# Two expert layers in a written order, with regrouped gather and scatter, contiguous weight loads, and attention products by halves

## The chip, the cores and the metric

The kernel runs on one core of a Trainium2 chip. The metric is the device time of one execution in microseconds (us); lower is better. TensorE is PE in the profile (its weight loads PEld), VectorE is DVE, ScalarE is ACT, GpSimd is POOL, and SyncE is SP, which issues most transfers. PE's clock is granted at one of two levels, 1.2 or 2.4 GHz; the profile shows the granted share of 2.4 GHz.

## What is computed

A sequence of 512 tokens of width 1024 goes through two layers of a first block and then through a second block. A layer of the first block is a mixer (grouped attention, a bidirectional state-space scan, differential attention and a spatial gate, joined by four gates), an expert layer, and a gated addition of a per-layer embedding (ple). The second block is a forgetting attention (fox), a convolutional feed-forward layer, a gated recurrence (hgrn) and a second feed-forward layer. The change is mostly in the expert layer:

```python
affinity = jax.nn.softmax((h @ w_router).astype(jnp.float32), axis=-1)
top_aff, idx = lax.top_k(jnp.swapaxes(affinity, 1, 2), cap)      # cap = 64 tokens for each of 16 experts
xe = h[bidx, idx]
hid = jax.nn.silu(jnp.einsum('becd,edf->becf', xe, w_gate_e)) * jnp.einsum('becd,edf->becf', xe, w_up_e)
ye = jnp.einsum('becf,efd->becd', hid, w_down_e)
return jnp.zeros_like(h).at[bidx, idx].add(ye * top_aff[..., None].astype(ye.dtype))
```

Each expert has three float32 matrices of 1024 x 1024, so a layer reads 48 of them, 192 MiB.

## The kernel before, in words

The activations lie in on-chip memory as eight tiles `x[j]` of 128 features by 512 tokens. Dense layers outside the experts split each float32 operand into a high and a low float32r part and sum three products, 512 columns wide. The expert matrices are multiplied in float32 without a split; the profile counts a float32 product as two records.

**Routing** (`route`, L1518). PE transposes the logits, DVE and ACT form the softmax, and DVE takes the 64 best tokens of each expert in eight rounds. Meanwhile PE turns `x` into token rows, and ACT scales them into eight tiles `ht[t, q]` (L1548). The result `pos_t` holds each token's slot at each expert.

**Pairs.** The experts go in eight pairs. `onehot(p)` (L1589) compares the slots with 1 to 64 and gives a 0/1 matrix of 512 tokens by 128 (two experts of 64). `gather` multiplies `ht` by it in float32: for each of eight feature chunks, four products of 128 columns. `product` (L1654) multiplies the gathered rows, 64 columns of stationary operand for each of the two experts e, with the matrices; the two experts write the two halves of PE's columns and run beside each other. Gate and up are 64 records each, and so are the two halves of down together (`half`, L1667). `down` (L1704) transposes the 0/1 matrix, weighs the result into a high and a low part (`yy`: ACT, then DVE), and scatters it: for each `x[j]`, two products of 512 columns and one addition by DVE (`add_x`).

**Loads.** `raw` (L1637) fetches 1 MiB at a time into a ring: 11 slots of `xraw`, 4 of `xraw2`, 2 of `raw`, and 3 that are used once, for loads 5 to 7 of a layer. A pair takes 24 loads, eight for each matrix kind. Gate and up loads take 256 rows of a matrix, so a partition gets two runs of 4 KiB; down loads take 512 rows of half the columns, four runs of 2 KiB. Before the last two downs the ring is closed and opened with 5 slots.

**Order.** `tc.manual_schedule()` keeps the program's order on every engine. In `moe` it covers only the routing and the first gather (L1586); behind it, a scheduler with its own cost estimates orders the instructions of each engine, so loads and small pieces move ahead of others. The mixer, `ple`, fox and hgrn are in a manual order that a planner writes (`Runner.go` with a `Clock` of estimated costs). `ple_early` (L1752) prepares products for the next stage and is a generator, advanced between the last halves of down.

**Attention.** `gqa` (L1059) builds operands by `halves`: a tile whose partitions 0 to 63 and 64 to 127 hold two parts of a head, copied by transfers on SP (`put`). A score is a 128-row product plus a 64-row one with the low part of k. In fox's `score` (L1881) each of two heads hh takes three 64-row products and a mask, first one head and then the other.

Of the kernel before, what the change touches and what calls it, by code (L numbers as in the profile page):

```python
# [21 lines left out]
S = 512  # L22
# [515 lines left out]
class Net:  # L538
# [520 lines left out]
    def gqa(self, i, aq, akv, rope):  # L1059
# [6 lines left out]
        for a, x in enumerate(tl):  # L1066
# [7 lines left out]
            st, low = self.halves(x, a == 0)  # L1074
            both.append(st)
            if a == 0:
                kl = low
            yield
        out = []
        sk, sq = both[0], both[1:]  # L1080

        def score(u):
            if u.qc == 0:
                u.g.po = self.psum("po")
            rows = slice(u.g.n * 64, (u.g.n + 1) * 64)
# [432 lines left out]
    def route(self, X, wk, t2k):  # L1518

        nc, ident, lg = self.nc, self.ident, X.lg  # L1520
        rt = lambda: t2k()[:NE]
        ps = self.xnorm_sums(X)
        zero = rt()
        nc.gpsimd.memset(zero, 0.0)
# [17 lines left out]
        def rows(t, q):  # L1542
# [8 lines left out]
        tq = [(t, q) for t in range(NT) for q in range(2)]  # L1551
        some = [(t, q, rows(t, q)) for t, q in tq[:2]]
# [5 lines left out]
        for t, q in tq[2:]:  # L1558
            normed(t, q, rows(t, q))
        aT = rt()  # L1560
# [6 lines left out]
        mk, cs = rt(), rt()  # L1567
        nc.vector.tensor_scalar(mk, aT, 0.0, None, op0=OP.is_lt)
        nc.vector.tensor_tensor_scan(cs, mk, zero, 0.0, op0=OP.add, op1=OP.add)
# [11 lines left out]
    def moe(self, i, X, nxt):  # L1581
        yield
        nc, I = self.nc, self.I
        with self.phase(X, {"mm": 4, "sm": 2, "po": 2}) as wk, self.work(f"ring_{X.name}", X.side) as px2, ExitStack() as top:
            t2k = lambda dt=F32: self.t(wk, [128, S], dt, "t2k", 11)
            with self.tc.manual_schedule():  # L1586
                af, ht, pos_t = self.route(X, wk, t2k)

                def onehot(p, n=1):  # L1589

                    o = t2k()
                    ov = o.rearrange("p (t e s) -> p t e s", t=NT, e=2)
                    for t in range(0, NT, NT // n):
                        sl = slice(t, t + NT // n)
                        nc.vector.tensor_tensor(ov[:, sl], pos_t[:, sl, 2 * p:2 * p + 2][:, :, :, None].to_broadcast([128, NT // n, 2, CAP]),
                                                self.c("slot")[:, None, None, :].to_broadcast([128, NT // n, 2, CAP]), op=OP.is_equal)
                    return lambda t: o[:, t * 128:(t + 1) * 128]

                def gather(i, oh, n=1):

                    xe = {}

                    def part(q, n=1):
                        ps = self.psum("sm")
                        for k in range(4):
                            for t in range(NT):
                                self.mm(ps[:, k * 128:(k + 1) * 128], ht[t, q][:, k * 128:(k + 1) * 128], oh(t),
                                        start=t == 0, stop=t == NT - 1)
                        x = xe[q] = t2k()
                        xv, pv = (v.rearrange("p (k c) -> p k c", k=4) for v in (x, ps))  # L1610
                        for k in range(0, 4, 4 // n):
                            sl = slice(k, k + 4 // n)
                            nc.vector.tensor_tensor(xv[:, sl], pv[:, sl], self.sm(f"g_moe{i}", 4 * q + k, 4 // n)[:, :, None].to_broadcast([128, 4 // n, 128]),
                                                    op=OP.mult)

                    def stat(k, e):
                        if k // 4 not in xe:
                            part(k // 4)
                        return xe[k // 4][:, (k % 4) * 128 + e * 64:(k % 4) * 128 + e * 64 + 64]
                    if n > 1:  # L1620
                        part(0, n)
                    return stat
                oh = onehot(0, 4)
                start = oh, gather(i, oh, 4)


            seq, once = [0, 0], range(5, 8)
            place = Box(pool=top.enter_context(self.work(f"first_{X.name}", X.side)))

            def settle():  # L1630
                top.close()
                place.pool = top.enter_context(self.work(f"late_{X.name}", X.side))
# [45 lines left out]
            def hidden(p):  # L1678
# [6 lines left out]
                if p == 0:  # L1685
                    settle()
# [608 lines left out]
```

## Time and profile before

| | |
|---|---|
| runs of before, median (lowest to highest) | 3641.29 us (3637.7 to 3650.09), 3 runs |
| the profiled execution, its time | 3644.31 us |
| its span | 3642.5 us |
| mean granted clock | 0.976 |
| PE busy | 3438.2 us (94%) |
| DVE, ACT, POOL busy | 1748.7 (48%), 1103.5 (30%), 276.5 (8%) |
| float32 products of the experts (four groups), busy by single records | 431.0 + 225.7 + 71.2 + 62.2 us |
| moved by transfers | 632.53 MB, mean 174 GB/s |

A busy PE means that some product is in flight; products overlap, so busy time is not the time at PE's peak. DMA share is the busy share of 16 transfer engines, and can read slightly over 1. In rows of windows the columns are: window, its length, then busy time (and instructions) of PE, PEld, DVE, ACT and POOL, then the granted clock, the DMA share and GB/s. L196 is the helper line through which every instruction goes, so groups are told apart by the tiles that they write and read (`mm`, `sm`, `po` are accumulators of the products, of gather and scatter, and of the transposes). The first expert layer lies at about 600 to 1130 us, the second at about 1740 to 2260 us, and fox at 2317 to 2615 us.

### The profile page before, as it was taken

How to read it: one execution, taken by the hardware profiler on the slowest of the kernel's cores; microseconds unless marked ns; L12 is line 12 of the kernel's file. 1: busy time of each engine (PE TensorE's matmuls, PEld its weight loads, DVE VectorE, ACT ScalarE, POOL GpSimd, SP SyncE). 2: the span in 40 equal slices, each digit the busy share in tenths (PEclk: the TensorE clock that was granted, in tenths of full speed). 3: DMA queues.
4: the chain of work that ended last, by engine and by line, in shares of the span. 5: the costliest groups of instructions: out<-in, count | busy, mean ns of one | idle time of the engine just before them, and what ended most of it. 6: DMA issues, size and time to landing. Idle time of an engine off the chain costs nothing.

```text
span 3642.5 us, 42086 instructions
## 1 busy us (share of the span) xinstructions
PE 3438.2 (94%) x17170; PEld 2422.3 (67%) x17170; DVE 1748.7 (48%) x2976; ACT 1103.5 (30%) x1754; POOL 276.5 (8%) x162
## 2 busy tenths in 40 slices
PE   7999878999999999988999999999999999999998
PEld 6787665434446777766444444777788888978887
DVE  4566853111116546764111113644565566667555
ACT  3443321000014344322000002444443344434333
POOL 0011320000001000221000000211100000000000
PEclk9999988999999999999999999999999999999999
DMA  5241336999983332236899986222222332213322
GB/s 158 81 129 60 102 124 260 386 382 403 397 334 99 103 90 88 83 97 255 315 378 397 392 347 219 88 76 73 67 94 93 104 94 80 64 64 100 98 93 81
DMA packets 346432, 632.53 MB, mean 174 GB/s; under 512 B 20008, under 2 KB 192552, under 8 KB 346240
## 3 DMA queue, kind: packets, MB, share of 16 engines
q1 hardware_dynamic: 330672, 613.53, 46.9%
q10 hardware_dynamic: 15568, 16.32, 1.5%
q8 instruction: 135, 2.21, 0.3%
q14 instruction: 57, 0.47, 0.0%
HBM read 618.15 MB, written 4.31 MB: 171 GB/s over the span
## 4 chain that ended last, share of the span: by engine, by line
PE 50%; DVE 5%; ACT 1%; issue 0%; DMA 0%; DVEq 0%; ACTq 0%
PE mm L196 41%; PE sm L196 3%; PE po L196 2%; PE s L196 1%; DVE x L196 1%; PE t L196 1%; DVE pl L196 1%; PE a L196 1%; DVE ach L196 1%; DVE w L196 0%; DVE t2k L196 0%; DVE sg L196 0%; ACT ach L196 0%; DVE P L196 0%; DVE yy L196 0%
## 5 line engine op out<-in xcount | busy, mean ns | idle before, releaser
L196 PE MATMUL mm<-ach,ph 128*128 128x512 f32 x5504 | 1751.1, 400 | 72.5 <-DVE w L196 46.4
L196 PEld LDWEIGHTS mm<-ach,ph 128*128 128x128 f32 x5504 | 1026.8, 191 | 317.3 <-issue 63.1
L196 PE MATMUL mm<-ach,pl 128*128 128x512 f32 x2752 | 1084.8, 394 | 0.6 <-DVE pl L196 0.5
L196 PEld LDWEIGHTS mm<-ach,pl 128*128 128x128 f32 x2752 | 523.7, 190 | 115.0 <-DVE pl L196 1.7
L196 ACT CAST ph<-raw 128x1024 fp32r<-128x1024 f32 (+1 forms) x366 | 373.6, 1030 | 301.7 <-PE mm L196 265.4
L196 PE MATMUL mm<-xraw,t2k 128*64 128x512 f32 x1840 | 431.0, 595 | 11.1 <-DVE t2k L196 11.1
L196 DVE TENSOR_TENSOR pl<-raw,ph 128x1024 fp32r<-128x1024 f32 (+1 forms) x317 | 390.6, 1235 | 96.7 <-ACT ph L196 94.7
L196 PEld LDWEIGHTS mm<-xraw,t2k 128*64 128x64 f32 x1840 | 140.0, 137 | 263.5 <-issue 234.0
L196 PE MATMUL mm<-xraw,hT 128*64 128x512 f32 x848 | 225.7, 598 | 0.0
L196 POOL TENSOR_TENSOR pl<-raw,ph 128x1024 fp32r<-128x1024 f32 x49 | 120.2, 2453 | 801.3 <-ACT ph L196 691.5
L196 DVE TENSOR_TENSOR t2k<-sm,small 128x512 f32<-128x512 f32 (+1 forms) x38 | 22.5, 606 | 307.0 <-PE mm L196 205.8
L196 ACT ACTIVATE w<-w 128x512 f32<-128x512 f32 x130 | 80.1, 629 | 283.8 <-DVE w L196 271.5
L196 ACT ACTIVATE sg<-mm 128x512 f32<-128x512 f32 x32 | 19.0, 597 | 416.9 <-PE mm L196 416.8
L196 PEld LDWEIGHTS sm<-t2k,t2k 128*128 128x128 f32 x1024 | 125.0, 203 | 21.8 <-issue 13.0
L196 PEld LDWEIGHTS mm<-xraw,hT 128*64 128x64 f32 x848 | 64.0, 136 | 109.7 <-issue 108.8
L196 PE MATMUL sm<-t2k,t2k 128*128 128x128 f32 x1024 | 130.9, 289 | 3.1 <-DVE t2k L196 1.6
L196 DVE SCALAR_TENSOR_TENSOR y<-u,small,y 128x512 f32<-128x512 f32 x176 | 131.9, 749 | 3.1
L196 DVE SCALAR_TENSOR_TENSOR yy<-mm,ac,yy 128x512 fp32r<-128x512 f32 x32 | 24.0, 751 | 220.4 <-ACT yy L196 220.4
L196 PE MATMUL sm<-oT,yy 128*128 128x512 f32 x256 | 90.9, 456 | 39.9 <-ACT yy L196 22.9
L196 DVE TENSOR_TENSOR sg<-sg,mm 128x512 f32<-128x512 f32 x32 | 21.9, 688 | 204.0 <-PE mm L196 204.0
L196 DVE TENSOR_TENSOR w<-mm,R 128x512 f32<-128x512 f32 x92 | 63.1, 688 | 113.9 <-PE mm L196 106.6
L196 POOL TENSOR_TENSOR w<-w,w 128x512 f32<-128x512 f32 x64 | 96.2, 1515 | 273.0 <-DVE w L196 263.4
(302 smaller groups left out, 3411.2 us busy)
## 6 DMA issues: line engine op xcount, KB each, us to landing
xraw<-in_w_exp_gate_dram SPq DMA_DIRECT2D x116, 1024.0 KB, 14.1
xraw<-in_w_exp_up_dram SPq DMA_DIRECT2D x114, 1024.0 KB, 18.5
xraw<-in_w_exp_down_dram SPq DMA_DIRECT2D x106, 1024.0 KB, 13.4
raw<-in_ffn_w_up_dram SPq DMA_DIRECT2D x44, 1024.0 KB, 5.1
raw<-in_w_branch_gate_dram SPq DMA_DIRECT2D x32, 1024.0 KB, 5.3
raw<-in_w_in_dram SPq DMA_DIRECT2D x22, 1024.0 KB, 5.4
raw<-in_w_exp_down_dram SPq DMA_DIRECT2D x22, 1024.0 KB, 11.0
raw<-in_ffn_w_down_dram SPq DMA_DIRECT2D x16, 1024.0 KB, 4.9
```

The source lines that it names most:

```text
L196: r = g(*a, **kw)
```

## The change

- The expert layer is in manual order throughout. The first 16 loads stand ahead of the routing in the program.
- The routing leaves `ht` as a high and a low float32r part (ACT scales, ACT copies, POOL subtracts), feature half by feature half.
- The 0/1 matrix covers four experts (256 columns), and the gather for two pairs is eight chunks of four times two float32r products of 256 columns.
- The scatter sums two pairs in one accumulation, so `add_x` comes half as often, and it stands behind the next gate product.
- The expert matrices are laid out so that a load of 1 MiB is one contiguous run of 8 KiB for each partition. Down goes through `product` except for the last pair.
- The ring has 1 slot of `xraw2` instead of 4; the once-used slots take loads 4 to 6; `ple_early` runs in one piece.
- gqa's second score product is 128 rows, from two more tiles (four more `put` transfers for each layer); fox's products alternate between the two heads.

```diff
-    def halves(self, x, twice):
-
-        h, l = self.parts(x)
+    def halves(self, x, order):
...
-        for g in range(2):
-            own, other = slice(g * 64, (g + 1) * 64), slice((1 - g) * 64, (2 - g) * 64)
-            o = self.w2k(F32R)
-            self.put(o[own], h[own])
-            self.put(o[other], (h if twice else l)[own])
-            out.append(o)
-        return out, l
+        for a, b in order:
+            row = []
+            for g in range(2):
+                own, other = slice(g * 64, (g + 1) * 64), slice((1 - g) * 64, (2 - g) * 64)
+                o = self.w2k(F32R)
+                self.put(o[own], parts[a][own])
+                self.put(o[other], parts[b][own])
+                row.append(o)
+            out.append(row)
+        return out
-            st, low = self.halves(x, a == 0)
-            both.append(st)
-            if a == 0:
-                kl = low
+            both.extend(self.halves(x, ((0, 1),) if a else ((0, 0), (1, 1))))
...
-        sk, sq = both[0], both[1:]
+        sk, sl, sq = both[0], both[1], both[2:]
...
                 self.mm(ps[r], q[:, cols], sk[u.g.n], start=True, stop=False)
-                self.mm(ps[r], q[rows, cols], kl[rows, :], start=False, stop=True)
+                self.mm(ps[r], q[:, cols], sl[u.g.n], start=False, stop=True)
...
-        def normed(t, q, ps):
-            o = ht[t, q] = t2k()
-            nc.scalar.activation(o, ps, AF.Identity, scale=r[:, t:t + 1])
+        def normed(q, t, ps):
+            h, l, f = t2k(F32R), t2k(F32R), t2k()
+            nc.scalar.activation(f, ps, AF.Identity, scale=r[:, t:t + 1])
+            nc.scalar.copy(h, f)
+            nc.gpsimd.tensor_tensor(l, f, h, op=OP.subtract)
+            ht[t, q] = h, l
...
-        with self.phase(X, {"mm": 4, "sm": 2, "po": 2}) as wk, self.work(f"ring_{X.name}", X.side) as px2, ExitStack() as top:
-            t2k = lambda dt=F32: self.t(wk, [128, S], dt, "t2k", 11)
+        with self.phase(X, {"mm": 4, "sm": 2, "po": 2}) as wk, self.work(f"ring_{X.name}", X.side) as px2, ExitStack() as top, \
+                self.tc.manual_schedule():
+            t2k = lambda dt=F32: self.t(wk, [128, S], dt, "t2k", 20)
...
+            seq, once = [0, 0], range(4, 7)
...
-                    return self.raw(src, nk, 2 * D // nk)
-                v = v.rearrange("p (k n) -> p k n", k=nk)
-                nc.sync.dma_start(v, src.rearrange("(k p) n -> p k n", p=128))
-                return v
-
+                    v = self.t(self.praw, [128, 2 * D], F32, "raw", bufs=self.RAW)
+                nc.sync.dma_start(v, src)
+                return v.rearrange("p (k n) -> p k n", k=nk)
+            def loads(w, p):
+                return [[raw(w[2 * p + e, kk], 2) for e in range(2)] for kk in range(4)]
...
-                    rv = [raw(w[2 * p + e][kk * 256:(kk + 1) * 256], 2) for e in range(2)]
+                    r = rv[kk] if rv else [raw(w[2 * p + e, kk], 2) for e in range(2)]
...
-                    rv = [raw(w[2 * p + e][kk * 512:(kk + 1) * 512, m * 512:(m + 1) * 512], 4) for e in range(2)]
+                    rv = [raw(w[2 * p + e, 2 * m + kk], 4) for e in range(2)]
...
+            first = [loads(I["w_exp_gate"][i], 0), loads(I["w_exp_up"][i], 0)]
+            af, ht, pos_t = self.route(X, wk, t2k, lambda: late([128, S], F32, "rt", 2))
+            def onehot(g, n=1):
+                o = self.t(wk, [128, NT, 4 * CAP], F32R, "oh", 1)
+                ov = o.rearrange("p t (e s) -> p t e s", e=4)
+                for t in range(0, NT, NT // n):
+                    sl = slice(t, t + NT // n)
+                    nc.vector.tensor_tensor(ov[:, sl], pos_t[:, sl, 4 * g:4 * g + 4][:, :, :, None].to_broadcast([128, NT // n, 4, CAP]),
+                                            self.c("slot")[:, None, None, :].to_broadcast([128, NT // n, 4, CAP]), op=OP.is_equal)
+                return o
...
+            def gather(b, oh):
+                ps = self.psum("sm")
+                pv = ps.rearrange("p (k c) -> p k c", k=2)
+                for k in range(2):
+                    q, c = divmod((2 * b + k) * 128, 512)
+                    for t in range(NT):
+                        for a, part in enumerate(ht[t, q]):
+                            self.mm(pv[:, k], part[:, c:c + 128], oh[:, t], start=t == 0 and a == 0, stop=t == NT - 1 and a == 1)
+                x = xe[b] = t2k().rearrange("p (k c) -> p k c", k=2)
...
+            def returns(g, oh):
+                for p in (2 * g, 2 * g + 1):
+                    o = lambda t: oh[:, t, p % 2 * 128:(p % 2 + 1) * 128].bitcast(F32)
+                    po = self.psum("po")
+                    for t in range(NT):
+                        nc.tensor.transpose(po[:, t * 128:(t + 1) * 128], o(t), self.ident)
+                    oT = late([128, S], F32R, "oT", 2)
+                    nc.scalar.copy(oT, po)
+                    pa = self.psum("po")
+                    for t in range(NT):
+                        self.mm(pa[:, :2], o(t), af[:, t, 2 * p:2 * p + 2], start=t == 0, stop=t == NT - 1)
+                    ac = self.t(wk, [128, 1], F32, "ac", 3)
+                    for e in range(2):
+                        nc.vector.tensor_copy(ac[e * 64:(e + 1) * 64], pa[e * 64:(e + 1) * 64, e:e + 1])
+                    back[p] = oT, ac
+            def scatter(j):
+                ps = self.psum("sm")
+                sl = slice(j % 4 * 128, (j % 4 + 1) * 128)
+                mms = [(part[:, sl], oT) for ys, oT in group for part in ys[j // 4]]
+                for q, (y, oT) in enumerate(mms):
+                    self.mm(ps, y, oT, start=q == 0, stop=q == len(mms) - 1)
+                self.add_x(j, ps)
+            def scatters():
+                for j in range(ND):
+                    scatter(j)
+                group.clear()
+            def gate(p, **kw):
+                sg = []
+                pgs = product(I["w_exp_gate"][i], p, rows_of(p), **kw)
                 if p == 0:
-                    oh, xe = start
-                else:
-                    oh = onehot(p)
-                    xe = gather(i, oh)
-                gp = product(I["w_exp_gate"][i], p, xe)
-                if p == 0:
+                    top.close()
+                    place.pool = top.enter_context(self.work(f"late_{X.name}", X.side))
...
+                return sg
+            def up(p, sg, **kw):
+                for s, pg in zip(sg, product(I["w_exp_up"][i], p, rows_of(p), **kw)):
+                    nc.vector.tensor_tensor(s, s, pg, op=OP.mult)
+            def turn(sg):
...
+            def weigh(p, m, py, ys):
+                yh, yl = (late([128, 512], F32R, "yy", 8) for _ in range(2))
+                nc.scalar.activation(yh, py, AF.Identity, scale=back[p][1])
+                nc.vector.scalar_tensor_tensor(yl, py, back[p][1], yh, op0=OP.mult, op1=OP.subtract)
+                ys[m] = yh, yl
+            NP = NE // 2
+            oh = onehot(0, 4)
+            gather(0, oh)
+            sg = gate(0, between=lambda kk: gather(kk + 1, oh) if kk < 3 else None, rv=first[0])
+            up(0, sg, rv=first[1])
+            for p in range(NP):
+                hT = turn(sg)
+                if p + 1 < NP:
+                    if p % 2:
+                        for b in range(4):
+                            gather(b, oh)
+                    sg = gate(p + 1)
+                    if p % 2 == 0:
+                        if group:
+                            scatters()
+                        returns(p // 2, oh)
+                        if p + 2 < NP:
+                            oh = onehot(p // 2 + 1)
+                    up(p + 1, sg)
+                if p == NP - 2:
 
                     X.close_ring()
                     nxt.begin()
                     X.open_ring(X.last)
-                    early = self.ple_early(i, nxt, raw, t2k)
-                    next(early)
-                down(p, *hid, early)
-                hid = nxt_hid
+                    for _ in self.ple_early(i, nxt, raw, t2k):
+                        pass
+                ys = {}
+                if p < NP - 1:
+                    group.append((ys, back[p][0]))
+                    for m, py in enumerate(product(I["w_exp_down"][i], p, hT)):
+                        weigh(p, m, py, ys)
+                    continue
+                self.clock.sync()
+                for m in range(2):
+                    weigh(p, m, half(I["w_exp_down"][i], p, hT, m), ys)
+                    if m == 0:
+                        scatters()
+                        group.append((ys, back[p][0]))
+                    for j in range(4 * m, 4 * m + 4):
+                        scatter(j)
+                        if j == ND - 2:
+                            X.close_ring()
+                            nxt.prime(1)
+                        nxt.chunk(j)
...
-            ps = []
+            ps = [self.psum("s") for _ in range(2)]
...
+            for m, o in ((0, 0), (0, 1), (1, 0)):
+                for hh in range(2):
+                    rows = slice(hh * 64, (hh + 1) * 64)
+                    self.mm(ps[hh][:, :n], q[m][rows, cols], k[o][rows, :n], start=m + o == 0, stop=False)
-                ps.append(p)
+                self.mm(ps[hh][:, n - 128:n], self.identb, maskb, start=False, stop=True)
...
+    for k in ("w_exp_gate", "w_exp_up", "w_exp_down"):
+        v = inp[k]
+        a[k] = v.reshape(2, NE, 4, 2, 128, D).transpose(0, 1, 2, 4, 3, 5).reshape(2, NE, 4, 128, 2 * D)
+        if k == "w_exp_down":
+            u = v[:, NE - 2:].reshape(2, 2, 2, 4, 128, 2, D // 2).transpose(0, 1, 5, 2, 4, 3, 6)
+            a[k] = np.concatenate([a[k][:, :NE - 2], u.reshape(2, 2, 4, 128, 2 * D)], 1)
+    a["w_ple"] = inp["w_ple"].reshape(2, 2, 128, D).transpose(0, 2, 1, 3).reshape(2, 128, 2 * D)
...
-        X.append(AheadMoe(net, f"e{i}", "left", "right", i, 11, 5, 4))
+        X.append(AheadMoe(net, f"e{i}", "left", "right", i, 11, 5, 1))
```

## Rows read from the trace of the kernel before

**Rows 1.** Second part of the page: busy tenths in 40 slices of the span.

```profile
PE   7999878999999999988999999999999999999998
DMA  5241336999983332236899986222222332213322
```

**Rows 2.** Windows of both layers, first expert product to last up product; columns as on the page.

```profile
608.00:1057.00 449.00, 426.29 (x2117) 187.61 (x2115) 69.40 (x116) 30.77 (x50) 0.00 (x0) 0.99 0.97 373
1743.00:2191.00 448.00, 424.96 (x2106) 186.49 (x2104) 68.25 (x112) 31.94 (x51) 0.00 (x0) 0.99 0.97 373
```

**Rows 3.** Chain that ended last, in order of time: start us, us, what; second layer.

```profile
1700.90 5.67 PE mm L196 x24
...
1742.92 7.02 PE mm L196 x32
...
1860.10 13.95 PE mm L196 x64
...
1912.29 2.88 PE sm L196 x24
...
1922.27 0.70 DVE t2k L196
...
1923.01 13.95 PE mm L196 x64
...
2170.25 20.89 PE mm L196 x96
```

**Rows 4.** Fifth part of the page: the scatter's products, both layers.

```profile
L196 PE MATMUL sm<-oT,yy 128*128 128x512 f32 x256 | 90.9, 456 | 39.9 <-ACT yy L196 22.9
```

**Rows 5.** Waits of SP's own queue, 1800 to 2160 us: total, times, longest.

```profile
SPq L196 <- PE mm L196: 176.2, 59, 13.4
```

**Rows 6.** Timeline of SP's queue: start us, us, transfers issued; second layer.

```profile
1672.76 12.98 SPq L196 DMA_DIRECT2D xraw<-in_w_exp_up_dram  x6
...
1713.00 1.39 SPq L196 DMA_DIRECT2D xraw<-in_w_exp_gate_dram  x3
...
1774.68 10.04 SPq L196 DMA_DIRECT2D xraw<-in_w_exp_down_dram  x3
```

**Rows 7.** Windows of 5 us in which those gate, up and down transfers ran.

```profile
1690.00:1695.00 5.00, 5.00 (x21) 3.20 (x20) 0.90 (x2) 0.63 (x1) 1.55 (x1) 1.00 1.02 409
1795.00:1800.00 5.00, 4.18 (x20) 1.21 (x18) 0.69 (x1) 0.00 (x0) 0.00 (x0) 1.00 1.05 385
```

**Rows 8.** Timeline of PE: two of a pair's small pieces, and 256-column float32r products.

```profile
1939.05 0.60 PE L196 MATMUL po<-cst,t2k 128*128 128x128 f32 x4
...
1940.59 1.05 PE L196 MATMUL po<-af,t2k 128*128 128x2 f32 x8
...
2471.33 0.40 PE L196 MATMUL mm<-ph,ach 128*128 128x256 f32 x2
...
2471.69 0.40 PE L196 MATMUL mm<-ph,ach 128*128 128x256 f32 x2
```

**Rows 9.** Timeline of DVE: the scan that ends the routing's selection, second layer.

```profile
1734.13 1.21 DVE L196 TENSOR_TENSOR_SCAN t2k<-t2k,t2k 16x512 f32<-16x512 f32 x1
```

**Rows 10.** Tile qk: POOL's float32r subtraction (ns min/median/max, first and last start).

```profile
L196 POOL TENSOR_TENSOR qk<-P,qk x8: 1277/1282/1738, 2328.6 to 2498.6; 128x512 fp32r<-128x512 f32 x8
```

**Rows 11.** Timeline of PE: forget-attention scores, and products that alternate row halves.

```profile
2482.74 0.55 PE L196 MATMUL s<-qk,qk 64*128 64x128 f32 x3
...
2498.87 0.96 PE L196 MATMUL s<-qk,qk 64*128 64x512 f32 x3
...
3030.26 1.05 PE L196 MATMUL a<-q,i 128*128 128x128 f32 x8
...
3031.68 1.16 PE L196 MATMUL u<-iv,ks 64*128 64x128 f32 x14
```

**Rows 12.** Windows of 5 us in which the granted clock fell.

```profile
1720.00:1725.00 5.00, 4.40 (x20) 3.53 (x20) 3.68 (x10) 2.94 (x5) 0.00 (x0) 0.50 1.02 413
1960.00:1965.00 5.00, 4.41 (x13) 2.65 (x14) 3.26 (x5) 0.00 (x0) 0.00 (x0) 0.70 1.02 409
```

More of the change, by code (lines that the diff above doesn't have):

```diff
@@ L1540, in route, with rows @@
         ht = {}
-        def rows(t, q):
+        def rows(q, t):
             ps = self.psum("sm")
@@ L1546, in rows @@
             return ps
-        def normed(t, q, ps):
-            o = ht[t, q] = t2k()
-            nc.scalar.activation(o, ps, AF.Identity, scale=r[:, t:t + 1])
-        tq = [(t, q) for t in range(NT) for q in range(2)]
-        some = [(t, q, rows(t, q)) for t, q in tq[:2]]
+        def normed(q, t, ps):
[4 more added lines that the diff above has]
+            ht[t, q] = h, l
+        qt = [(q, t) for q in range(2) for t in range(NT)]
+        some = [(q, t, rows(q, t)) for q, t in qt[:2]]
         pt = self.psum("po")
@@ L1557, in route @@
             normed(*v)
-        for t, q in tq[2:]:
-            normed(t, q, rows(t, q))
-        aT = rt()
+        for q, t in qt[2:]:
+            normed(q, t, rows(q, t))
+        aT = put()[:NE]
         for k in range(CAP // 8):
@@ L1583, in moe @@
         nc, I = self.nc, self.I
-        with self.phase(X, {"mm": 4, "sm": 2, "po": 2}) as wk, self.work(f"ring_{X.name}", X.side) as px2, ExitStack() as top:
-            t2k = lambda dt=F32: self.t(wk, [128, S], dt, "t2k", 11)
[L1586 to L1627, printed above, removed]
@@ L1676, in half @@
                 return pg
-            def hidden(p):
-                if p == 0:
-                    oh, xe = start
-                else:
-                    oh = onehot(p)
-                    xe = gather(i, oh)
-                gp = product(I["w_exp_gate"][i], p, xe)
-                if p == 0:
-                    settle()
-                sg = []
-                for m in range(2):
-                    s = late([128, S], F32, "sg", 3)
-                    nc.scalar.activation(s, gp[m], AF.Silu)
-                    sg.append(s)
-                up = product(I["w_exp_up"][i], p, xe)
+            first = [loads(I["w_exp_gate"][i], 0), loads(I["w_exp_up"][i], 0)]
@@ L1693, in hidden @@
+            def turn(sg):
                 hT = []
-                for m in range(2):
-                    nc.vector.tensor_tensor(sg[m], sg[m], up[m], op=OP.mult)
+                for s in sg:
                     ps = self.psum("po")
                     for b in range(4):
-                        nc.tensor.transpose(ps[:, b * 128:(b + 1) * 128], sg[m][:, b * 128:(b + 1) * 128], self.ident)
-                    h = late([128, 4, 128], F32, "hT", 3)
+                        nc.tensor.transpose(ps[:, b * 128:(b + 1) * 128], s[:, b * 128:(b + 1) * 128], self.ident)
+                    h = late([128, 4, 128], F32, "hT", 2)
@@ L1738, in moe @@
-            hid = hidden(0)
-            early = None
-            for p in range(NE // 2):
-                nxt_hid = hidden(p + 1) if p + 1 < NE // 2 else None
-                if p == NE // 2 - 2:
+                return lambda k, e: hT[k // 4][:, k % 4, e * 64:(e + 1) * 64]
+            def weigh(p, m, py, ys):
[3 more added lines that the diff above has]
+                ys[m] = yh, yl
```

69 lines of the change are left out of this document (17 added, 52 removed).

## The prediction

> **What bounds the kernel now.** I read the 40 slices first. PE is at 8 to 9 tenths almost everywhere, and the transfer engines reach 8 to 9 tenths in two places only: slices 6 to 11 and 18 to 23, the two expert layers [rows 1]. Since the change is mostly there, I took windows from each layer's first expert product to its last up product: 449 and 448 us, PE busy for 425 of them, a transfer share of 0.97 at a mean of 373 GB/s, clock 0.99 [rows 2]. So both resources are nearly full, and the question is which is really the bound.
>
> The chain of waits runs through PE alone there, with no transfer as a link: gather pieces (`sm`), products (`mm`), and short links of DVE and ACT [rows 3]. A pair of experts takes 62.9 us, from one up product at 1860.10 to the next at 1923.01 [rows 3]. SP's own queue spends 176 of 360 us waiting for a PE product to free a slot [rows 5]. So PE is the bound.
>
> But the transfers are hardly below it. When six up loads (runs of 4 KiB) had just been issued at 1672.76, the next windows moved 409 GB/s at share 1.02; when down loads (runs of 2 KiB) ran, 385 at share 1.05 [rows 6, 7]. A load is 1.0486 MB, so 2.56 and 2.72 us, and a pair's 16 and 8 loads need 62.8 us: the pair's 62.9 again. So taking work from PE gives almost nothing by itself; the transfers take over at once. How fast a load of the new layout is decides the size of the gain.
>
> **The change, part by part.** I sum for one layer, from the first expert product to the end of the last up product, before: 1742.92 to 2170.25 + 20.89 = 2191.14, 448 us [rows 3].
>
> *PE's work in this stretch afterwards.* A product of 64 records is 13.95 us [rows 3]; there are 16 gate and up and 6 down: 307. Gather: a float32r product of 256 columns follows the last after 0.12 us (three from 2471.33 to 2471.69) [rows 8], and four experts need 8 x 4 x 2 = 64: 7.7 us for two pairs, where before 64 records at 0.12 (24 in 2.88 [rows 3]) served one pair and 0.70 us of DVE followed. Three groups and half of the first fall in the stretch: 27. Transposing the 0/1 matrix and weighing, 0.60 + 1.05 [rows 8], eight times: 13. The eight transposes of the hidden rows, twice 0.60, seven times: 8. Scatter: 5.67 / 24 = 0.236 us for a product of 512 columns [rows 3], 32 for each of three groups of four: 23. Sum 378 us, 52.3 for a pair. The scatter's idle time, 39.9 us in both layers, mostly behind ACT's and DVE's weighing [rows 4], goes too: the scatter now stands a gate product of 14 us later, and four products (0.94 us) cover one addition of about 0.7.
>
> *The transfers' work.* Through the last up product a layer needs 16 x 8 + 8 x 6 = 176 loads. The ring holds 11 + 1 + 2 + 3 = 17 before PE consumes any. PE's first gate product now has two gathers inside, 14 + 3.8 = 18 us; until its end only loads 17 to 20 find free slots (load 21 reuses load 7's, which goes last). So 155 loads remain after 18 us, the queue is never empty again (14 slots are 35 us of transfers, PE's longest stretch without loads is gather, scatter and returns, some 18), and the last load needs about 2 us of PE.
>
> What is one load of 8 KiB runs? No row shows one. Nearest is 4 KiB: 2.56 us. From 2 to 4 KiB the time fell by 0.16; were that a fixed cost for each run, halving again gives 0.08 less, 2.48. I take 2.53 between; the other end is 2.72, if the new address pattern is as slow as the slowest row. Then 18 + 155 x 2.53 + 2 = 412 us, and PE's 378 fit below it. Gain 36 a layer (43 at 2.48, 31 at 2.56, 6 at 2.72): **-72** for two.
>
> The Trainium skill ("DMA: Bandwidth & Descriptors", "Why small descriptors are slow (HBM only)") gives a packet a fixed overhead of about 3 cycles beside one cycle for 32 bytes. By it 4 to 8 KiB would bring 1.2%, an estimate of 414 GB/s and 2.53 us; it would also make 2 to 4 KiB worth 2.3%, and the trace shows 6% (385 to 409), so it understates what the rows show.
>
> *Before the first product.* The wider 0/1 matrix and 32 gather products (3.8 us at 0.12) stand where 32 records of 0.12 stood: 0. At half clock, as seen at 1720 [rows 12], they double, +4. The split of the token rows is new: POOL's eight subtractions at 1.28 [rows 10] take 10 us, hidden by DVE's selection, which ends at 1735.34 [rows 9]; the second feature half isn't needed before the third gather. SP is in program order now: load 4 waits for a slot that came free at 1713.00 [rows 6], and loads 5 to 16 stand behind it; 13 loads end by 1746, while load 4 is first needed some 10 us after the first product. I take 0; ends -1 and +4.
>
> *After the last up product.* PE's pieces are the same. `ple_early` is now one piece: 48 products at 0.236 = 11 us, with four waits for ACT and DVE to split (DVE's 0.70 as in [rows 3] and about as much of ACT, 1.3 us each) that other work used to fill. Meanwhile transfers bring the last downs. **+4** for two layers; ends -6 and +16.
>
> *Fox.* A triple of products is 0.55 us at 128 columns and 0.96 at 512 [rows 11]; by pitch (0.12 at 256, 0.236 at 512) a triple adds 0.27, 0.36, 0.53 and 0.71 at the four widths, 1.87 for a head, and for eight pairs of heads 15 us are saved if one head hides the other wholly. Products that alternate row halves are in the trace: 14 in 1.16 us, against 8 full ones in 1.05 [rows 11], 0.083 against 0.131, 37% less. That of 30 us is 11. PE isn't always what is awaited there: **-9**; ends -15 and +2 (DVE receives both heads late).
>
> *gqa.* Products keep their width. Four more transfers on SP at 0.46 [rows 6] delay the weights behind them by 1.9 us a layer at most; PE has a loaded slot as cover: **+2**; ends 0 and +6.
>
> *Sum.* -72 + 4 - 9 + 2 = -75. The profiled execution took 3644.3 with a span of 3642.5; that makes 3569. The median of the runs is 3.0 below that execution: **3566 us**.
>
> **Rivals.**
>
> 1. *Runs of 8 KiB bring nothing.* For it: no row shows one, and each transfer engine now reads in another pattern. Against: longer runs were faster in the one step that can be seen. At 2.72 us a layer gains 6 to 8: about -15 + 4 - 9 + 2 = -18, **3623**.
> 2. *PE stays the bound, and its relief counts in full.* For it: before, a pair's summed pieces (52.3 + 3.9 of gather + stalls of about 3) are below its 62.9, so unseen costs exist. It decides if a load is faster than 2.38 us. With 12 us of small waits, 390: -58 a layer, **3522**.
> 3. *Slower: PE idles for transfers and its clock falls.* Place: the product phases, where PE needs 3.5 us for two loads that take 5.1, so a gap follows every 16 records. After idle stretches the granted clock was 0.50 in the routing and 0.70 at 1960 [rows 12], though elsewhere in the layer gaps left it at 1.00. With a share f of the work at 1.2 GHz a pair is 52.3 (1 + f): it exceeds the transfers' 60.7 at f = 0.16 and the present 62.9 at f = 0.20, the point from which it decides. At 0.25 a pair is 65.4, +2.5 for some seven pairs, +36 for two layers: **3674**. Against: while PE lags, its gaps close, and full slots wait for it.
>
> The Trainium skill ("TensorE: Matmul & The Clock Gate", "Loop structure matters more than you think") warns of this loop: a long transfer wait before each product leaves PE cold. By that rule the third rival holds. The trace agrees for the routing's gaps and not for the short ones of the layer, whose mean clock is 0.99 [rows 2].
>
> **How the numbers follow.** The forecast has 0.73 (its own range 3535 to 3600), rival 1 0.12, rival 2 0.08, rival 3 0.07, of which I put 0.03 near its deciding point, where nothing changes. I count 0.3%, 11 us, as what can be told from no change. Forecast and rivals 1 and 2 are faster; with a little of rival 1 left inside, faster 0.90, same 0.05, slower 0.05. The range reaches to rival 1 and short of rival 2: 3530 to 3622.
>
> **What would show it.** Right: a rate of 410 to 422 GB/s at full share through both layers; waits of PE's products for `xraw`, which hardly exist now; 60 to 61.5 us a pair; 405 to 420 us from first product to last up product; 0.12 us for a gather product; no idle time before the scatter; 8 to 15 us less in fox. Wrong: a pair at 62 us or more, a rate under 400, a clock under 0.9 in the layers, or SP waiting for PE as it does now.

## The result and the profile after

| | before | after |
|---|---|---|
| median of runs (lowest to highest) | 3640.73 us (3637.7 to 3650.09), 4 runs | 3554.19 us (3551.47 to 3558.19), 4 runs |
| ratio after to before | | 0.9756 [0.9737, 0.9775] |
| profiled execution, its span | 3644.31, 3642.5 us | 3555.33, 3553.5 us |
| first expert product to end of last up product, both layers | 448.0, 448.3 | 419.7, 419.8 |
| router's transpose to first expert product | 26.9, 26.0 | 25.9, 25.4 |
| end of last up product to the next dense product | 69.1, 67.6 | 71.0, 72.7 |
| fox, start of the first to start of the last score product | 213.1 | 187.5 |
| moved, in packets | 632.53 MB in 346432 | 633.53 MB in 264893 |

Faster by 86.5 us, 12 us more than forecast and well inside the range. The stretches are read from the timeline of PE, by the start of the first and the end of the last product that names them (fox from start to start). In the page's slices the transfer engines now stand at 9 tenths in both layers, where they were at 8 to 9 [rows 1], and the rate is a flat 420 GB/s:

```profile
PE   7999878998988999989999988999999999999998
DMA  5242325999993332233999994222233232222222
GB/s 174 77 128 66 101 92 233 416 420 420 420 366 93 102 96 85 78 95 133 392 420 420 420 411 174 91 78 91 66 103 97 93 99 73 73 69 95 95 97 81
```

The windows of both layers of after, which answer to [rows 2], and behind them four of 5 us in the first layer. Mean rate 411 for 373; PE's busy time falls from 426 to 388. The short ones show a hole in the transfers 14 to 24 us into the stage, and a product phase in which PE is busy 3.67 of 5 us at full clock:

```profile
601.00:1021.00 420.00, 388.37 (x1881) 165.00 (x1881) 52.59 (x86) 31.36 (x53) 0.00 (x0) 0.99 1.00 411
1707.00:2127.00 420.00, 386.40 (x1883) 163.19 (x1882) 52.37 (x85) 30.66 (x52) 0.00 (x0) 1.00 1.00 412
615.00:620.00 5.00, 5.00 (x26) 1.59 (x24) 0.00 (x0) 1.19 (x2) 0.00 (x0) 1.00 0.42 169
620.00:625.00 5.00, 5.00 (x26) 1.72 (x24) 0.00 (x0) 0.00 (x0) 0.00 (x0) 1.00 0.80 257
625.00:630.00 5.00, 5.00 (x26) 1.69 (x24) 0.00 (x0) 0.00 (x0) 0.00 (x0) 1.00 1.00 421
985.00:990.00 5.00, 3.67 (x18) 1.19 (x16) 0.00 (x0) 0.00 (x0) 0.00 (x0) 1.00 1.01 416
```

SP's own waits, 1765 to 2120 us (total, times, longest): where it waited 176.2 us for PE [rows 5], it now waits 38.3, and for the transfers before it:

```profile
SPq L196 <- DMA xraw<-in_w_exp_gate_dram: 85.7, 39, 4.6
SPq L196 <- DMA xraw<-in_w_exp_up_dram: 74.2, 36, 2.1
SPq L196 <- DMA xraw<-in_w_exp_down_dram: 73.2, 37, 2.1
SPq L196 <- PE mm L196: 38.3, 38, 13.5
```

On PE the products now wait for loads, and the scatter's idle time falls from 39.9 [rows 4] to 12.3 us, where the prediction had none (groups of PE's instructions, both layers, three of them):

```profile
L196 PE MATMUL mm<-xraw,t2k 128*64 128x512 f32 x1776 | 461.1, 601 | 28.2 <-DMA xraw<-in_w_exp_gate_dram 21.2 <-DMA xraw<-in_w_exp_up_dram 7.0
L196 PE MATMUL mm<-xraw,hT 128*64 128x512 f32 x848 | 218.8, 599 | 26.6 <-DMA xraw<-in_w_exp_down_dram 26.6
L196 PE MATMUL sm<-oT,yy 128*128 128x512 f32 x256 | 70.3, 417 | 12.3 <-DVE x L196 10.1 <-ACT yy L196 1.6 <-DVE yy L196 0.6
```

PE's timeline of after at the end of the first layer's stage (start, us, what, idle time before it): 16 records in 3.65 us (two rows show 14, for records can be missing), then 1.33 us for a load, 4.98 us from one to the next, so 2.49 us a load. Then the scatter takes 8 us, and from there PE waits for no load:

```profile
972.02 3.65 PE L196 MATMUL mm<-xraw,hT 128*64 128x512 f32 x14 [1.33 <-DMA xraw<-in_w_exp_down_dram]
...
986.99 3.65 PE L196 MATMUL mm<-xraw,t2k 128*64 128x512 f32 x16 [1.33 <-DMA xraw<-in_w_exp_gate_dram]
991.97 3.65 PE L196 MATMUL mm<-xraw,t2k 128*64 128x512 f32 x14 [1.33 <-DMA xraw<-in_w_exp_gate_dram]
995.55 8.05 PE L196 MATMUL sm<-oT,yy 128*128 128x512 f32 x32
```

### The profile page after: what moved, and what is told of

It reads as the page before. It is cut to its first block, busy times and chain, and to the rows that moved or that the text cites. A ratio compares the mean times of both kernels' runs of the same rounds, so it can differ in the third digit from the quotient of the medians.

```text
span 3553.5 us, 41092 instructions
## 1 busy us (share of the span) xinstructions
PE 3308.3 (93%) x16658; PEld 2345.6 (66%) x16658; DVE 1708.9 (48%) x2914; ACT 1103.9 (31%) x1770; POOL 295.6 (8%) x176
## 2 busy tenths in 40 slices
DMA packets 264893, 633.53 MB, mean 178 GB/s; under 512 B 20136, under 2 KB 192680, under 8 KB 215296
## 4 chain that ended last, share of the span: by engine, by line
PE 42%; DMA 9%; DVE 4%; ACT 1%; issue 0%; SPq 0%; DVEq 0%; ACTq 0%
PE mm L196 36%; DMA xraw<-in_w_exp_down_dram 3%; DMA xraw<-in_w_exp_gate_dram 2%; PE po L196 2%; DMA xraw<-in_w_exp_up_dram 2%; PE sm L196 1%; PE t L196 1%; PE s L196 1%; PE a L196 1%; DVE x L196 1%; DVE pl L196 1%; DVE ach L196 1%; DMA raw<-in_w_exp_up_dram 1%; DMA raw<-in_w_exp_gate_dram 1%; DVE w L196 0%
## 5 line engine op out<-in xcount | busy, mean ns | idle before, releaser
L196 PE MATMUL mm<-xraw,t2k 128*64 128x512 f32 x1776 | 461.1, 601 | 28.2 <-DMA xraw<-in_w_exp_gate_dram 21.2
L196 ACT ACTIVATE yy<-mm,ac 128x512 fp32r<-128x512 f32 x32 | 22.0, 687 | 419.8 <-PE mm L196 419.8
L196 PE MATMUL mm<-raw,t2k 128*64 128x512 f32 x272 | 124.1, 608 | 2.6 <-DMA raw<-in_w_exp_gate_dram 2.6
L196 DVE TENSOR_TENSOR x<-x,sm 128x512 f32<-128x512 f32 x80 | 54.2, 685 | 137.4 <-PE sm L196 137.4
L196 DVE TENSOR_TENSOR x<-x,mm 128x512 f32<-128x512 f32 x80 | 54.4, 684 | 122.1 <-PE mm L196 122.1
```

The costliest lines, as they stand in the source:

```text
L196: r = g(*a, **kw)
```

## The experiments

Each was timed beside the kernel before on its chip, except where one run is named; three chips were used, so ratios to before are compared, and not medians (after: 0.9756 [0.9737, 0.9775], once more 0.9755). Three dots mark what is left out of an edit. "Stage" is the stretch from first expert product to the end of the last up product.

**1. After, with runs of 4 and 2 KiB.**

```diff
-                nc.sync.dma_start(v, src)
+                nc.sync.dma_start(v, src.rearrange("(k p) n -> p k n", p=128))
...
```

> The changed kernel with the expert matrices (and w_ple) as they lay before: runs of 4 KiB for gate and up, for the downs of all but the last pair runs of 4 KiB too, and of 2 KiB for the last pair; all else as changed. Theory T (after PE's relief the transfers are the bound of the expert layers, and the longer runs set their pace): the rate falls from 420 to about 409 GB/s, a load from 2.49 to 2.56 us, so the 172 loads behind the routing take 12 to 13 us more in a layer (up to 21 if it is nearer to the 386 of the short runs), 3579 us (3572 to 3600). Rival P (PE's smaller work alone shortened the layers, the runs don't matter): 3554, within 8.

3578.92 us, 0.9816 [0.9801, 0.983], as theory T had it; stage 431.0 and 429.8 us, 11 and 10 longer than after. **2. Before, with the contiguous layout alone** (the same edit the other way):

> The kernel before with only the layout changed: each load of 1 MiB is a run of 8 KiB for each partition; order, gather and scatter as before. Theory T: PE is the bound there, 62.9 us for a pair, so it stays near 3640: at most 10 us less in a layer, where a late transfer held PE (3620 to 3643). Rival L (the long runs alone made the gain of the layers, some 28 us each): about 3584.

3645.32 us, 1.000 [0.999, 1.0009]; stage 448.2 and 447.1. So the runs alone bring nothing: before, PE was the bound. But the rest of the change, without the runs of 8 KiB, brings 17.0 and 18.5 of the 28 us a layer, and the prediction had said that taking work from PE "gives almost nothing by itself". Not all of that need be PE's relief: in the first experiment the down loads of all but the last pair are runs of 4 KiB too, where before had 2 KiB. By [rows 7] that is 0.16 us a load, for 48 loads up to 8 us of transfers a layer (an estimate), and no run separates it. Three windows each of before, of this first experiment and of after show where the time went: up to the end of the second down product, up to the sixth, and the rest.

```profile
608.00:763.00 155.00, 149.81 (x745) 64.13 (x743) 21.05 (x37) 10.33 (x17) 0.00 (x0) 0.99 0.93 358
763.00:1016.00 253.00, 237.75 (x1169) 104.17 (x1168) 41.35 (x68) 17.35 (x29) 0.00 (x0) 0.99 1.03 400
1016.00:1057.00 41.00, 38.72 (x204) 19.31 (x204) 7.00 (x11) 3.09 (x5) 0.00 (x0) 1.00 0.71 262
```

```profile
602.00:739.00 137.00, 129.87 (x652) 52.47 (x651) 12.61 (x21) 9.09 (x16) 0.00 (x0) 1.00 1.00 392
739.00:986.00 247.00, 217.10 (x1041) 92.57 (x1040) 31.58 (x51) 16.46 (x28) 0.00 (x0) 0.99 1.03 409
986.00:1033.00 47.00, 42.45 (x192) 18.98 (x192) 8.15 (x15) 5.94 (x10) 0.00 (x0) 0.96 0.97 384
```

```profile
601.00:735.00 134.00, 129.07 (x649) 52.25 (x650) 12.46 (x21) 8.95 (x16) 0.00 (x0) 1.00 0.98 399
735.00:976.00 241.00, 218.64 (x1044) 94.37 (x1045) 31.99 (x51) 16.87 (x29) 0.00 (x0) 0.98 1.01 420
976.00:1021.00 45.00, 40.66 (x192) 18.38 (x190) 8.13 (x16) 5.54 (x10) 0.00 (x0) 1.00 0.98 403
```

In the middle the two paces were nearly equal: 253 and 247 us for four pairs, and the last stretch loses those 6 us again. The 18 us are won in the first two pairs, where a full ring of slots stands ready: there PE's busy time falls from 149.8 to 129.9 us, and its first wait of over 1 us for a load comes at 719.82, 118 us into the stage. So we read it that PE sets the pace until it has used up that stock. The runs of 8 KiB then shorten the middle, by 6 us to 241, and the two ends by 3 and 2.

**3. Fox undone.**

```diff
...
+            for hh in range(2):
...
+                for m, o in ((0, 0), (0, 1), (1, 0)):
+                    self.mm(p[:, :n], q[m][rows, cols], k[o][rows, :n], start=m + o == 0, stop=False)
+                self.mm(p[:, n - 128:n], self.identb, maskb, start=False, stop=True)
...
```

> The changed kernel with the forget attention's score products as before, all of one head and then all of the other. Theory F (the order of the halves alone is the gain of that stage: products of the two row halves run beside each other and hide each other's weight loads; the chain's share of them was 52 us before and about 26 after): 3554 + 25 = 3579 (3572 to 3584). The prediction's term: + 9, 3563; the rest of the stage's gain would then come from another order of the planner.

3581.25 us, 0.983 [0.9812, 0.9847]: by the ratios fox is worth 27 us, with some 9 either way, and its stretch takes 213.2 us again, 25.7 more. **10. Head 0's products ahead of head 1's, both masks last** tells what in it:

```diff
-            for m, o in ((0, 0), (0, 1), (1, 0)):
-                for hh in range(2):
+            for hh in range(2):
+                for m, o in ((0, 0), (0, 1), (1, 0)):
```

> Fox with both heads' accumulators open and both masks last, as after the change, but with the three products of head 0 ahead of the three of head 1. Theory A (what the change brought in fox is that products which alternate between the row halves hide each other): it is lost again, about 3579 us (3575 to 3585). Rival M (it is the place of the masks and the two open accumulators): 3554 us (3550 to 3558). In between, both have a share.

3559.86 us, 0.9767 [0.9754, 0.978]: 4 us above after on the same chip (0.9755), inside the intervals, and fox takes 187.6 us, as in after (187.5). Theory A falls; it is the masks' place, with both heads' accumulators open, and no run separates these two. PE's timeline of one unit of two heads at 512 columns, first with fox undone, then in turn:

```profile
2341.89 0.96 PE L196 MATMUL s<-qk,qk 64*128 64x512 f32 x3
2342.79 0.23 PE L196 MATMUL s<-maskb,identb 128*128 128x128 bf16 x1
2342.95 0.96 PE L196 MATMUL s<-qk,qk 64*128 64x512 f32 x3
2343.84 0.23 PE L196 MATMUL s<-maskb,identb 128*128 128x128 bf16 x1
2344.00 0.66 PE L196 MATMUL po<-pT,v 128*64 128x128 f32 x8
```

```profile
2341.45 0.97 PE L196 MATMUL s<-qk,qk 64*128 64x512 f32 x6
2342.36 0.28 PE L196 MATMUL s<-maskb,identb 128*128 128x128 bf16 x2
2342.57 0.66 PE L196 MATMUL po<-pT,v 128*64 128x128 f32 x8
```

Six products take what three took: the heads run wholly beside each other, in both orders of issue that were run, when no product of all 128 rows stands between them. A unit falls from 2.11 us (2341.89 to 2344.00) to 1.12; over the 32 units (eight of each width) the sum falls from 51.6 to 27.4 (27.2 after).

**4. gqa's second score product on 64 rows again.**

```diff
-                self.mm(ps[r], q[:, cols], sl[u.g.n], start=False, stop=True)
+                self.mm(ps[r], q[rows, cols], kl[rows, :], start=False, stop=True)
...
```

> The changed kernel with gqa as before (a 128-row product and then a 64-row one, four copies fewer in a layer). Theory G (a 64-row product next to 128-row ones can't hide its weight load: four products took 1.67 us before and 1.07 after, 8 times in each of two layers): + 9.6 us, 3564 (3559 to 3568). The prediction's term (the width of the product doesn't matter, the copies cost 2): 3552.

3564.76 us, 0.9772 [0.9757, 0.9787]: 6 us above after by the ratios, and the intervals overlap, so the time shows nothing by itself. The timeline is clearer: two products of 128 rows and two of 64, then the same four all of 128 rows (after):

```profile
106.92 1.69 PE L196 MATMUL s<-w,w 128*128 128x512 f32 x4
108.54 0.73 PE L196 MATMUL mm<-ach,ph 128*128 128x512 f32 x2
```

```profile
107.27 1.07 PE L196 MATMUL s<-w,w 128*128 128x512 f32 x4
108.18 0.61 PE L196 MATMUL mm<-ach,ph 128*128 128x512 f32 x2
```

From the unit's start to the next product: 1.62 and 0.91 us. Over the sixteen units that is 25.7 us for 16.2, and gqa from its first unit to the product behind its last takes 50.9 and 49.8 us in the two layers for 44.9 and 47.4 after (44.9 and 45.8 in the second trace of after): 8 to 10 us. It looks like the same thing as in fox: where products on 64 and on 128 rows take turns, one follows the other after 0.40 us (a quarter of 1.62), and after 0.23 where all have 128 rows. That both have one cause is our reading of these units.

**5. The gather's products run twice.**

```diff
+                    for _ in range(2):
...
```

> The gather's 32 products of each pair of expert groups are run twice over, into the same sums' place, so that the result is the same and TensorE alone has about 7.7 us more per two groups (some 31 us a layer). Theory T (the transfers set the pace of the expert stage after the change, TensorE waits for them 1.3 us between products): the added work goes into those waits, about +4 us a layer at the start and end of the stage, 3560 us, at most 3570. Rival P (TensorE still sets the pace, the waits for transfers are only what came last by the records): the added work counts in full, +30 us a layer, about 3615.

3571.47 us, 0.9795 [0.9777, 0.9813], 14 us by the ratios. The stage grows by 3.7 us in both layers; the other 4 a layer come before it (router to first product 29.7 and 30.1 us), where two of each layer's gathers stand with nothing to cover them, and which the expectation had left out. PE's waits of this run in the second layer's stage (total, times, longest) are 7.5 and 3.8 us for gate and down loads; they were 10.8 and 13.3 after.

```profile
PE mm L196 <- DMA xraw<-in_w_exp_gate_dram: 7.5, 7, 1.3
PE mm L196 <- DMA xraw<-in_w_exp_down_dram: 3.8, 3, 1.3
```

In the stage the transfers set the pace, so rival P falls: of some 27 us more of PE's work (an estimate: 224 more products at 0.12), 3.7 show. A further relief of PE would thus have little left to give there.

**6. The scatter of the three later groups ahead of the gate products.**

```diff
-                    sg = gate(p + 1)
...
                         if group:
                             scatters()
-                        returns(p // 2, oh)
+                            returns(p // 2, oh)
+                            sg = gate(p + 1)
...
```

> For the three later pairs of expert groups the scatter (8 us of products) stands ahead of the next gate products instead of between them and the up products. Theory (TensorE is 8 to 10 us behind the last load at the end of the stage because the scatter stands just before the last up products): both layers end about 5 us earlier, 3544 us, between 3540 and 3554. Rival (what follows the stage, the next block's own loads and additions, sets its end): no change, 3554.

3551.02 us, 0.974 [0.9726, 0.9753]; stage 415.1 and 415.8 us, 4 to 5 shorter as expected. The way from there to the next dense product, 74.5 and 73.1 us, tells nothing, for with the same code it takes 71.0 to 74.3 in other runs. In time it is 6 us by the ratios, whose intervals overlap, so the gain is shown by the stages alone.

**7. That, and the block behind the stage in turn; 11. the same once more; 8. after once more, beside it.** `ple_early` transposes row block b + 1 ahead of the sums of block b, and its table is loaded ahead of the last weights.

```diff
+        nx = cut(0)
+        for b in range(4):
+            h, l = nx
+            nx = cut(b + 1) if b < 3 else None
...
```

> The kernel with the scatter ahead of the gate products, and besides it the block after the expert stage put in turn (the transposes of one row block's products ahead of the sums of the block before), its table loaded ahead of the last weights. Theory: the 1.2-us stalls of that block (some 8 of them in a layer) and the wait for its table go, 3 to 6 us a layer below the kernel with the scatter alone, about 3535 us (3528 to 3545). Rival (these stalls are covered by the transfers that the next mixer waits for): the time of the kernel with the scatter alone, 3544.

> The kernel after the change once more, as the reference for the two versions of this call on the same chip: 3554 us, between 3549 and 3560.

> The version with the scatter ahead of the gate products and the block behind the stage put in turn, once more, beside the kernel after the change on the same chip: 3541 us, 10 to 16 us below it, if the first measurement holds; the same time as it if that was the chip's.

3541.58 us, 0.9708 [0.969, 0.9726]; once more 3539.8, 0.9714 [0.9701, 0.9727], beside after at 3556.24, 0.9755 [0.974, 0.9771]. This version beats both kernels, after by 15 to 16 us. Its stage is 416 us, and from there to the next dense product it takes 67.3 us where after takes 71 to 73. What the turn and what the earlier table brings of this wasn't run separately. The block in PE's timeline, after and then this version:

```profile
1023.30 2.56 PE L196 MATMUL po<-t2k,t2k 128*128 128x512 f32 x10 [0.70 <-DVE t2k L196]
1027.05 3.29 PE L196 MATMUL po<-t2k,t2k 128*128 128x512 f32 x12 [1.19 <-ACT t2k L196]
1031.53 3.30 PE L196 MATMUL po<-t2k,t2k 128*128 128x512 f32 x12 [1.19 <-ACT t2k L196]
1036.03 3.29 PE L196 MATMUL po<-t2k,t2k 128*128 128x512 f32 x12 [1.19 <-ACT t2k L196]
```

```profile
1022.33 12.34 PE L196 MATMUL po<-t2k,t2k 128*128 128x512 f32 x46 [0.71 <-DVE t2k L196]
1034.60 1.94 PE L196 MATMUL mm<-raw,hT 128*64 128x512 f32 x8
```

**12. That, and the first loads in an order in which none waits for a slot ahead of one that needn't.**

```diff
-            seq, once = [0, 0], range(4, 7)
+            seq, once = [0, 0], range(13, 16)
...
```

> As the kernel with scatter ahead and the tail in turn, and besides it the first weight loads of a layer in an order in which none that must wait for a buffer stands ahead of one that needn't: the last three of the first sixteen loads get buffers of their own. Theory (about 10 us of transfers are lost at the start of the stage because the queue's program waits for load 4's buffer until 573 us, and about 8 at the end): the stage ends some 14 us earlier a layer than after the change, about 3526 us (3520 to 3540). Rival (the transfers ahead of the stage take their share from the mixer's own): the start brings nothing, the time of the kernel with the tail alone, about 3535.

3543.19 us, 0.9712 [0.9699, 0.9725]; stage 415.7 and 415.9, where the version before it has 416.0 and 416.1: nothing, my theory of the start falls. The ring is now full early (rate 1 from 592 to 604), but the hole only moves, with the first product at 604.60:

```profile
592.00:604.00 12.00, 6.77 (x36) 6.61 (x37) 6.79 (x14) 1.50 (x2) 0.84 (x1) 0.52 0.00 1
620.00:625.00 5.00, 5.00 (x26) 1.65 (x24) 0.00 (x0) 1.19 (x2) 0.00 (x0) 1.00 0.70 247
625.00:630.00 5.00, 5.00 (x26) 1.65 (x24) 0.00 (x0) 0.00 (x0) 0.00 (x0) 1.00 0.49 182
```

**9. After, with two slots fewer at the start.**

```diff
-            seq, once = [0, 0], range(4, 7)
+            seq, once = [0, 0], range(4, 5)
```

> The kernel after the change with two slots of the ring fewer at a layer's start (15 instead of 17: the second and third of the once-used slots are left out). Theory R (what holds the transfers back in the first 25 us of a stage is that every slot of the ring is full until TensorE has finished the first gate product; from there on they run without a stop): two loads fewer stand ready at that point, so the stage from its first product to its last up product is 2 x 2.49 = 5 us longer in each layer, 424.7 us for 419.7. Rival S (the queue's program order alone holds them back): no change, 419.7.

One run, 3562.26 us; stage 423.0 and 422.9, 3.2 more for the 5 expected of theory R and the 0 of S. Read through the slots, in both kernels load 22 (counted from 0) reuses a slot that the first up product frees, and so it does in the twelfth. SP's queue issues it and load 23 21.9, 21.8 and 21.8 us after the first product (600.91, 601.02 and 604.60) in after, in this run and in the twelfth, whatever the ring held before:

```profile
622.79 0.80 SPq L196 DMA_DIRECT2D xraw<-in_w_exp_gate_dram  x2
622.83 0.80 SPq L196 DMA_DIRECT2D xraw<-in_w_exp_gate_dram  x2
626.41 0.80 SPq L196 DMA_DIRECT2D xraw<-in_w_exp_gate_dram  x2
```

Fewer slots only leave more of the loads before it to be done in the hole (347 GB/s from 605 to 625 us, 280 after). So slots it is, but with the ring's order of reuse in it, not their number alone.

## Why the prediction was right, and its terms

| term | predicted | measured |
|---|---|---|
| stage, each layer | -36 | -28.2, -28.5 |
| before the first product, each | 0 | -1.0, -0.7 |
| after the last up product, both | +4 | +7 (+5 in the second trace of after) |
| fox | -9 | -25.6 in the trace, 27 by undoing it |
| gqa | +2 | -8 in the trace, -10 in the second trace of after |

The measured terms sum to -85, and the span fell by 89; in the second trace of after they sum to -88, and the span fell by 98. The rest lies in stretches that no term names. The mechanism of the stage was right: PE was the bound, and the transfers of 8 KiB runs became it. Of the signs, the rate (420 GB/s), the stage, a pair in the middle (241 / 4 = 60 us) and 0.12 us for a gather product came as said; the scatter kept 12.3 us of idle time, and fox gave 25.6 us for the 8 to 15. Rival 1 (long runs bring nothing) is refuted by the rate of 420 and by the first experiment, rival 2 (PE stays the bound) by the doubled gather. Rival 3 had its gaps, 1.33 us behind 3.65 in the product phases, and behind these the granted clock stayed at 1.00, the level of 2.4 GHz. It fell to 0.50, 1.2 GHz, four times in the two stages of after, for 3.4 us each: at 766.4, 889.2 and 1872.3 us behind the transposes of the 0/1 matrix and the 2-column products, and at 872.2 us behind the longest wait for a load, 2.53 us, while one of 2.38 us in the second layer, and one of 2.60 us in the first layer of the ninth run, left it at 1.00 (window as above, then PE's timeline):

```profile
870.00:875.00 5.00, 2.83 (x8) 0.99 (x10) 0.00 (x0) 0.00 (x0) 0.00 (x0) 0.72 1.00 415
872.17 5.33 PE L196 MATMUL mm<-xraw,t2k 128*64 128x512 f32 x14 [2.53 <-DMA xraw<-in_w_exp_gate_dram]
```

In before there were four such falls too, and three of 3.4 us in a stage of 420 are a share of 0.02, where rival 3 needs 0.20; so its price never came due. The Trainium skill ("TensorE: Matmul & The Clock Gate", "Loop structure matters more than you think") warns of a long transfer wait ahead of each product; with waits of 1.33 us the trace doesn't show that loss.

The sentence that taking work from PE gives almost nothing by itself was wrong, and the prediction's own sum says so: 31 us a layer at 2.56 us a load. The first experiment has such loads, and the sum with the steps below, 25 + 155 x 2.56 + 3.65 + 5.1, gives 430.6 for its 431.0 and 429.8. What the sentence left out, as we read the windows, are the loads that stand ready when the stage begins.

The first step that was off is the stage, forecast at 18 + 155 x 2.53 + 2 = 412 and measured at 419.7:
- A load took 2.49 us, not 2.53: -6.2.
- Loads run without a stop from 25 us on, not from 18. Load 159, behind which PE waited at 972.02, landed 371.1 us after the first product; with 139 loads of 2.49 us behind load 20 that leaves 25. The step let load 22 follow when the gate product ends; it needs a slot that the first quarter of the up product frees, and is issued at 21.9 us. +7.
- The last load's own products take 3.65 us, not 2: +1.7.
- The scatter stands ahead of the last up product, so that PE is late there: 419.7 against 25 + 155 x 2.49 + 3.65 = 414.6, +5.1. With the scatter moved the stage was 415.1 and 415.8, so this part is shown.

The second is fox. The prediction took 15 us, by pitch, as the gain of full overlap, and kept 11 and then 9 of them, because products on alternating halves elsewhere were 37% quicker. Three parts of that failed. The heads overlap wholly, as the six products in 0.97 us show. Alternation isn't what brings it, for the tenth experiment has none and loses nothing. And the pitch left out what the mask costs: three products take 0.96 by the row and 0.71 by pitch, which we read as the mask letting nothing run on beside them. PE was what fox waits for, for the whole sum of the units came out in time (24.4 of 25.6).

The third is gqa, priced by the width of its products alone: the step took their rows to cost nothing, and got the sign wrong. The Trainium skill ("TensorEngine Tiling (Array Packing)", "Key Properties") states that tiles of the array work independently, and that a change of the tiling drains the engine. Both readings agree with it: 64-row products with a 128-row one between them, in fox 2.11 us a unit and 1.12 without, in gqa 1.62 and 0.91.

So the time came out 12 us below the forecast because two errors of some -17 and -10 outweighed +15 in the stages and +3 behind them. That it came so near is in part luck: the stages gave 57 of the 72 us, and fox and gqa, forecast at 7 together, gave 34 to 36.

## What to carry to other kernels

Where two resources are level in the middle of a stage, look at its ends too: a stock of loaded slots lets the relieved engine gain at the start, and a piece of other work just before the last products can end up in the time (5 of the scatter's 8 us here). Count for each slot which product frees it, not how many there are. On PE, group products by the rows that they use: here two halves ran beside each other in both orders of issue, and with a full-height product between them they did not.

## What the runs showed of the hardware

- Transfers of 1 MiB with one run of 8 KiB for each partition held 420 GB/s from 735 to 976 us, and with runs of 4 KiB 409 from 739 to 986 us (first experiment); loads of 2 KiB runs showed 385 [rows 7].
- Six 64-row products of two heads, on the two halves of the rows, took 0.97 us, and three of one head 0.96.
- PE's granted clock stayed at 1.00 behind waits of 1.33 us in product phases with 27% idle time (3.67 of 5 us busy), and fell to 0.50 for 3.4 us behind one of 2.53 us, but not behind one of 2.60 us in the ninth run.
